# Reversing the tile order of the second half of the tokens at both ends of a stage

## The chip, the cores and the metric

The kernel runs on one core of a Trainium2 chip. The metric is the device time of one launch in microseconds. Before the change it is 2606.45 us, the median of 3 runs from 2605.48 to 2608.71. Engines are named TensorE (PE, with its weight loads as PEld), VectorE (DVE), ScalarE (ACT), GpSimd (POOL) and SyncE (SP), which issues the DMAs.

## The reference

One inference step of a decoder trunk of two layers, in float32, for 512 prompt tokens and 8 sample tokens that share the weights. Each layer is a half-step SwiGLU FFN, a token mixer with three parallel branches, and a second FFN, each with a residual and a layer norm:

```python
def _layer(x, prev, n_prev_valid, lb, p):
    x = _layernorm(ALPHA * x + 0.5 * _swiglu(x, p['ffn1_wg'], p['ffn1_wu'], p['ffn1_wd']), p['ln1_g'], p['ln1_b'])
    y, new_state = _mixer(x, prev, n_prev_valid, lb, p)
    x = _layernorm(ALPHA * x + y, p['ln2_g'], p['ln2_b'])
    x = _layernorm(ALPHA * x + 0.5 * _swiglu(x, p['ffn2_wg'], p['ffn2_wu'], p['ffn2_wd']), p['ln3_g'], p['ln3_b'])
    return x, new_state
```

The model width is 1024, the FFN's 2816. In the mixer one projection `h = x @ w_in + b_in` feeds sliding-window attention, a Mamba-2 scan and HGRN2 (a gated recurrence with 4 heads of 128, in chunks of 64 tokens), and three gates. The branches' gated results are summed and projected by `w_out`. The new states are outputs too.

## The kernel before, in words

Activations lie with features on the 128 partitions and 520 tokens along the free axis: a tensor of 1024 features is 8 tiles of 128 x 520. The tokens go in two halves of 260 (`HALVES`). A product of a 128 x 128 weight block and 260 tokens keeps float32 accuracy by splitting both sides into a high and a low part: three matmuls (L177, L178, L179 in `gemm`). A unit of weights is 128 x 1024: one DMA of 512 KB into `ws`, a cast to the high part `wh` on ScalarE (L90), a subtraction for the low part `wl` on VectorE (L91). `ws`, `wh` and `wl` have 5 buffers each, and `get` issues two units ahead of the one in use. One unit against one half of the tokens is 24 products.

A stage is an FFN or a mixer. At its end (`ln_tail`) all 8 output tiles are made for half 0 and then all 8 for half 1, so that the layer norm of half 0 runs while TensorE is at half 1; each of the 8 weight units is therefore loaded twice. The next stage begins in the same way: the FFN takes its first HEAD = 4 gate and up tiles for half 0 and then for half 1 (`halves_head`), the mixer its first ten units of `w_in` (`MIX_HEAD`). The layer norm of half 1 is kept back in `open_ln` and is finished inside the head (`ln_rest`: after the second gate product of an FFN, after the third unit of a mixer). `ln_apply` then writes the normed activations tile by tile: a subtraction on GpSimd (L248), a scaling on VectorE (L249), the high part `xh` on ScalarE (L252), the low part `xl` on VectorE (L253). The FFN's second kind of gate and up product (`gate_up`, matmuls L409 to L411) needs sums of activations, made by `combine` (VectorE L379, L387, L388, L393, GpSimd L380, ScalarE L392; results `sx`), and pairs of units from which VectorE (L102, L103) and GpSimd (L104, L105) make sums that are then cast and split (L73, L74). The values of a head pass through L318 to L320.

In the mixer, units 0 to 3 of `w_in` are the forget gates `hT` of the four HGRN heads (evacuated at L517), units 4, 5 and 6 the query, input and output gate of head 0, 7 to 9 those of head 1, 10 to 15 those of heads 2 and 3. After the mixer's head the rest comes in rounds, woven with the HGRN heads (`weave`, `HG_ROUNDS` = 0, 2, 4, 5). A head (`hgrn_head`) takes two sigmoids of its `hT` (L639, L640), cumulated products of eight on GpSimd, scaled queries `hep` and keys `hk` (L660, L661), then five levels, each a small group of four matmuls (L678) and multiplications on VectorE (L697, L698, L705, L706); transpositions of `hi` and `hk` (L717), states `hst` (L724, L725, L728), the output products (L735, L738), a reciprocal root by Newton steps on four columns (L262 to L267, `newton`), `ho` (L746), its transposition (L754) and `hy` (L756), cast to `yhh` (L535). The merge of the HGRN branch multiplies `yhh`.

The order on each engine is set by a list scheduler with a model of times: instructions are emitted in program order with priorities (`EARLY`: weights and evacuations before the rest), and each engine then runs its list in order.

Of the kernel before, what the change touches and what calls it, by code (L numbers as in the profile page):

```python
# [37 lines left out]
TAIL = 8  # L38
# [4 lines left out]
HEAD = 4  # L43
# [82 lines left out]
class Kernel:  # L126
# [59 lines left out]
    def ln_add(self, half, n, end=False):  # L186
        nc = self.nc
        c0, c1 = HALVES[half]
        w = c1 - c0
        y = self.y[n][:, c0:c1]  # L190
        s1, s2 = self.s1[half][:, :w], self.s2[half][:, :w]
        if n == 0:
# [8 lines left out]
        nc.vector.tensor_tensor(s1, self.y[0][:, c0:c1] if n == 1 else s1, y, op=ALU.add)  # L201
        if not end:
            nc.gpsimd.tensor_tensor(s2, s2, sq, op=ALU.add)

# [79 lines left out]
    def ffn_units(self, l, f):  # L284
        for j0, n in FFN_GROUPS:
            head = self.halves_head() if j0 == 0 else []
            for j, half in head:
                self.w.add(self.ap["w_gu"][l, f, j0 + j, 0], DT, P)
                self.w.add(self.ap["w_gu"][l, f, j0 + j, 1], DT, P)
            for j in range(HEAD if j0 == 0 else 0, n):  # L290
                self.w.add_pair(self.ap["w_gu"][l, f, j0 + j, 0], self.ap["w_gu"][l, f, j0 + j, 1])
            for m, half in self.halves_last(j0 + n == NFT):
                self.w.add(self.ap["w_dn"][l, f, m, :, j0 * P : (j0 + n) * P], n, P)

    @staticmethod
    def halves_head():

        return [(j, (0,)) for j in range(HEAD)] + [(j, (1,)) for j in range(HEAD)]

    @staticmethod  # L300
    def halves_last(last):

        if not last:
            return [(m, (0, 1)) for m in range(DT)]
        k = DT - TAIL
        return [(m, (0, 1)) for m in range(k)] + [(m, (0,)) for m in range(k, DT)] + [(m, (1,)) for m in range(k, DT)]

    def ffn(self, l, f, g, b, last=False, then=None):
        nc = self.nc
        sx = None  # L310
        for j0, n in FFN_GROUPS:
            hid = [(self.out_slot(F32R, "hh"), self.slot(F32R, "hl")) for _ in range(n)]

            def hidden(j, half, s, up):

                c0, c1 = HALVES[half]
                h, (hh, hl) = s, hid[j]
                nc.vector.scalar_tensor_tensor(h, up, 0.5, s, op0=ALU.mult, op1=ALU.mult)  # L318
                nc.scalar.copy(hh[:, c0:c1], h)
                nc.vector.tensor_tensor(hl[:, c0:c1], h, hh[:, c0:c1].bitcast(F32), op=ALU.subtract)  # L320

            for j, halves in self.halves_head() if j0 == 0 else []:
                wg, wu = self.w.get(), self.w.get()
                for half in halves:
                    pg, pu = self.bank(), self.bank()
                    self.gemm(pg, wg, self.xs, half)
                    if sx is None and j == 1:
                        self.ln_rest()
                        sx = self.combine()
                    self.gemm(pu, wu, self.xs, half)  # L330
                    with self.early(1):
                        s = self.half_tile()
                        nc.scalar.activation(s, pg[:, :TA], AF.Silu)
                        hidden(j, half, s, pu[:, :TA])
            self.gate_up(range(HEAD if j0 == 0 else 0, n), sx, hidden)
            if j0 == 0 and then:
                then()
            fin = j0 + n == NFT
            if j0 == 0:
                self.new_y()  # L340

            def down(m, wt, half):
                c0, c1 = HALVES[half]
                w = c1 - c0
                p = self.bank()
                self.gemm(p, wt, hid, half)
                y = self.y[m][:, c0:c1]
                with self.early(1):
                    if j0 == 0:
                        self.residual(m, half, p)  # L350
                    else:
                        nc.vector.tensor_tensor(y, y, p[:, :w], op=ALU.add)

            if not fin:
                for m, halves in self.halves_last(False):
# [100 lines left out]
    def ln_tail(self, step, g, b, bd, last=False):  # L456
        self.ln_begin(0)
        self.ln_begin(1)
        for m, halves in self.halves_last(True):
            wt = self.w.get()  # L460
            for half in halves:
                step(m, wt, half)
                with self.early(2):
                    self.ln_add(half, m, last and half == 1 and m == DT - 1)
                if m == DT - 1:
                    end = lambda half=half: self.ln_end(half, g, b, split=not last, out=self.ap["y"] if last else None)
                    if half == 0 or last:
                        end()
                    else:
                        self.open_ln = end  # L470
        y = self.y
        self.raw = (lambda n, half: y[n][:, slice(*HALVES[half])]), b, bd


    def mixer_units(self, l):
        w, ap = self.w, self.ap

        def win(*us):
            for u in us:
                w.add(ap["w_in"][l, u], DT, P)  # L480

        def branch(r):
# [12 lines left out]
        branch(2)  # L495
        for m, halves in self.halves_last(True):
            w.add(ap["w_out"][l, m], DT, P)

# [8 lines left out]
    def lin(self, evac, m=P, halves=(0, 1)):  # L507
        wt = self.w.get()
# [7 lines left out]
    def lin_bias(self, out, bias, scale=1.0, halves=(0, 1)):  # L516
        self.lin(lambda p, c0, c1: self.nc.scalar.activation(out[:, c0:c1], p, AF.Identity, bias=bias, scale=scale), halves=halves)  # L517

    def lin_silu(self, out, hbias, halves=(0, 1)):
# [10 lines left out]
        self.lin(evac, halves=halves)  # L530

    def split(self, y, name, slot=None):
        nc = self.nc
# [67 lines left out]
    def hgrn_lin(self, l):  # L601
# [2 lines left out]
        T = [self.slot(name="hT") for _ in range(HGH)]  # L604
        q, it, sg = {}, {}, {}

        def unit(u, halves=(0, 1)):
            hb = dp[:, u : u + 1]
            if u < 4:
                self.lin_bias(T[u], pr[:, 48 + u : 49 + u], halves=halves)  # L610
                return
            h, kind = (u - 4) // 3, (u - 4) % 3
            d, n = ((q, "hq"), (it, "hi"), (sg, "hsg"))[kind]
            if h not in d:
                d[h] = self.slot(name=n)
            if kind == 1:
                self.lin_bias(d[h], pr[:, 48 + u : 49 + u], halves=halves)
            else:
                self.lin_silu(d[h], hb, halves)

        for half in (0, 1):
            for u in self.MIX_HEAD:
                unit(u, (half,))
                if half == 0 and u == 2:
                    self.ln_rest()
        yield T, q, it, sg
        for u in range(16):
            if u in self.MIX_HEAD:
# [915 lines left out]
```

## Time and profile before

| | |
|---|---|
| Median of 3 runs | 2606.45 us (2605.48 to 2608.71) |
| The profiled execution's own time | 2604.06 us |
| Its span from first to last instruction | 2602.3 us |
| Mean granted clock of TensorE | 0.992 |
| TensorE busy | 2543.6 us, 98% of the span |
| VectorE busy | 1949.4 us, 75% |
| ScalarE, GpSimd busy | 48%, 27% |
| DMA | 314.86 MB in the main queue, 36.3% of 16 engines |
| Weight units of one kind (L90, L91) | 382 |

The busy shares are averages over stages with different limits. An engine's row in a view of stretches tells how full it is there, and the granted clock tells whether TensorE ran at its upper level. A timeline row has its start, its duration, the instruction's engine, line and tiles, and in brackets how long the engine stood idle before it and what released it. In a timeline a matmul of two float32 operands that are not split is counted twice, and neighbouring instructions of one line share a row.

### The profile page before, as it was taken

What the parts mean: (1) busy time and instruction counts of PE and PEld (TensorE: products, weight loads), DVE (VectorE), ACT (ScalarE), POOL (GpSimd) and SP (SyncE); (2) the same over time, 40 slices, a digit from 0 to 9 for tenths busy, and PEclk for the clock granted to TensorE, in tenths of its full rate; (3) what the DMA queues carried; (4) which work ended last, traced back from release to release, by engine and by line L of the source; (5) the groups of instructions that cost most, each with busy time, mean ns of one, the idle gap of its engine ahead of it and who ended that gap; (6) DMA issues with size and microseconds to landing.
All of it is one profiled execution on the core that took longest, in us unless ns stands there. A gap on an engine that the chain in (4) does not pass through costs nothing.

```text
span 2602.3 us, 51878 instructions
## 1 busy us (share of the span) xinstructions
PE 2543.6 (98%) x20784; PEld 2474.7 (95%) x20784; DVE 1949.4 (75%) x3690; ACT 1250.4 (48%) x2358; POOL 694.6 (27%) x635
## 2 busy tenths in 40 slices
PE   8999999999999999999999999999999999999997
PEld 8999999898989999999989999999989899999997
DVE  8795988864685598868897858989546845978586
ACT  6352566443534473434663524764435344635255
POOL 1121243300143441212331212433001434413124
PEclk9999999999999999999999999999999999999999
DMA  6332356412242343232532414564123423333233
GB/s 208 105 122 82 127 178 217 149 68 83 99 141 91 122 138 106 90 114 82 186 128 93 141 55 150 171 219 145 57 84 112 139 90 122 138 98 107 89 125 119
DMA packets 134066, 318.17 MB, mean 122 GB/s; under 512 B 20452, under 2 KB 56516, under 8 KB 133824
## 3 DMA queue, kind: packets, MB, share of 16 engines
q1 hardware_dynamic: 133824, 314.86, 36.3%
q8 instruction: 163, 2.67, 0.4%
q14 instruction: 79, 0.65, 0.1%
HBM read 302.93 MB, written 11.88 MB: 121 GB/s over the span
## 4 chain that ended last, share of the span: by engine, by line
PE 73%; DVE 15%; DMA 4%; issue 3%; ACT 3%; POOL 3%; SPq 0%; POOLq 0%; ACTq 0%; DVEq 0%
PE g L177 15%; PE g L178 15%; PE g L179 15%; PE g L409 5%; PE g L411 5%; PE g L410 5%; DVE wl L91 3%; PE s L409 2%; PE s L411 2%; PE s L410 2%; DMA ws<-in_w_gu 1%; PE s L1130 1%; DVE y L249 1%; DMA smp<-r8d 1%; DVE xl L253 1%
## 5 line engine op out<-in xcount | busy, mean ns | idle before, releaser
L177 PE MATMUL g<-xh,wh 128*128 128x260 f32 (+1 forms) x2336 | 669.1, 287 | 7.5 <-ACT xh L1407 5.7
L178 PE MATMUL g<-xl,wh 128*128 128x260 f32 (+1 forms) x2336 | 668.7, 286 | 3.6 <-DVE xl L253 2.7
L179 PE MATMUL g<-xh,wl 128*128 128x260 f32 (+1 forms) x2336 | 668.2, 286 | 1.9 <-DVE wl L91 1.9
L90 ACT CAST wh<-ws 128x1024 fp32r<-128x1024 f32 (+1 forms) x382 | 389.9, 1024 | 376.6 <-PE g L178 252.4
L91 DVE TENSOR_TENSOR wl<-ws,wh 128x1024 fp32r<-128x1024 f32 (+1 forms) x382 | 469.4, 1231 | 117.4 <-ACT wh L90 116.6
L177 PEld LDWEIGHTS g<-xh,wh 128*128 128x128 f32 (+1 forms) x2336 | 439.5, 188 | 17.5 <-issue 6.1
L178 PEld LDWEIGHTS g<-xl,wh 128*128 128x128 f32 (+1 forms) x2336 | 439.2, 188 | 12.0 <-issue 4.2
L179 PEld LDWEIGHTS g<-xh,wl 128*128 128x128 f32 (+1 forms) x2336 | 439.6, 188 | 9.5 <-issue 4.1
L73 ACT CAST wh<-ws 128x1024 fp32r<-128x1024 f32 (+1 forms) x288 | 265.4, 942 | 295.9 <-PE g L178 161.7
L179 PE MATMUL g<-hh,wl 128*128 128x260 f32 x1408 | 396.1, 283 | 0.0
L178 PE MATMUL g<-hl,wh 128*128 128x260 f32 x1408 | 396.0, 283 | 0.0
L177 PE MATMUL g<-hh,wh 128*128 128x260 f32 x1408 | 391.8, 282 | 1.6 <-DVE y L275 1.6
L74 DVE TENSOR_TENSOR wl<-ws,wh 128x1024 fp32r<-128x1024 f32 (+1 forms) x288 | 320.3, 1118 | 87.1 <-ACT wh L73 86.0
L105 POOL TENSOR_TENSOR ws<-ws 128x512 f32<-128x512 f32 x72 | 136.2, 1892 | 632.0 <-DMA ws<-in_w_gu 260.0
L177 PEld LDWEIGHTS g<-hh,wh 128*128 128x128 f32 x1408 | 263.0, 188 | 2.1 <-DVE y L275 2.0
L178 PEld LDWEIGHTS g<-hl,wh 128*128 128x128 f32 x1408 | 264.7, 188 | 0.1
L179 PEld LDWEIGHTS g<-hh,wl 128*128 128x128 f32 x1408 | 264.6, 188 | 0.2
L409 PE MATMUL g<-xh,wh 128*128 128x260 f32 x864 | 246.3, 286 | 2.6 <-ACT wh L73 2.5
L410 PE MATMUL g<-xl,wh 128*128 128x260 f32 x864 | 245.0, 284 | 0.0
L411 PE MATMUL g<-xh,wl 128*128 128x260 f32 x864 | 242.4, 284 | 1.9 <-DVE wl L74 1.9
L409 PEld LDWEIGHTS g<-xh,wh 128*128 128x128 f32 x864 | 164.4, 190 | 4.8 <-ACT wh L73 3.7
L409 PE MATMUL g<-sx,wh 128*128 128x260 f32 x576 | 164.7, 286 | 4.3 <-ACT wh L73 4.3
(407 smaller groups left out, 5721.6 us busy)
## 6 DMA issues: line engine op xcount, KB each, us to landing
ws<-in_w_gu SPq DMA_DIRECT2D x208, 512.0 KB
ws<-in_w_in SPq DMA_DIRECT2D x132, 512.0 KB
ws<-in_w_dn SPq DMA_DIRECT2D x96, 512.0 KB
ws<-in_w_out SPq DMA_DIRECT2D x32, 512.0 KB
ws<-in_w_dn SPq DMA_DIRECT2D x32, 384.0 KB
smp<-r8d SPq DMA_DIRECT2D x48, 256.0 KB
ws<-in_w_br SPq DMA_DIRECT2D x24, 512.0 KB
smp<-in_hgr SPq DMA_DIRECT2D x16, 256.0 KB
```

What stands on the lines that cost most here:

```text
L73: nc.scalar.copy(h[:, :n], s[:, :n])
L74: nc.vector.tensor_tensor(lo[:, :n], s[:, :n], h[:, :n].bitcast(F32), op=ALU.subtract)
L90: nc.scalar.copy(h[:, :n], s[:, :n])
L91: nc.vector.tensor_tensor(lo[:, :n], s[:, :n], h[:, :n].bitcast(F32), op=ALU.subtract)
L105: nc.gpsimd.tensor_tensor(pa[:, b], u[:, a], u[:, b], op=ALU.add)
L177: nc.tensor.matmul(out, lhsT=h[:, wc], rhs=xh[:, c0:c1], start=st, stop=False)
L178: nc.tensor.matmul(out, lhsT=h[:, wc], rhs=xl[:, c0:c1], start=False, stop=False)
L179: nc.tensor.matmul(out, lhsT=lo[:, wc], rhs=xh[:, c0:c1], start=False, stop=en)
L249: nc.vector.scalar_tensor_tensor(y, y, gn, rb, op0=ALU.mult, op1=ALU.mult)
L409: nc.tensor.matmul(out, lhsT=h[:, wc], rhs=xh, start=first and k == 0, stop=False, **go)
L410: nc.tensor.matmul(out, lhsT=h[:, wc], rhs=xl, start=False, stop=False, **go)
L411: nc.tensor.matmul(out, lhsT=lo[:, wc], rhs=xh, start=False, stop=k == HK - 1, **go)
```

## The change

In the second half of the tokens the tiles are taken in reverse order, both in the tails and in the heads (`there_and_back`). The last tile of half 0 is then the first of half 1, and its weights are kept instead of loaded again: the last pair of units in an FFN's head (`held` = 1), the last two units in a tail and in a mixer's head (`held` = 2). The sums of the layer norm follow the order in which the tiles come (`seen`). The units to be loaded fall from 382 to 358; the matmuls stay the same.

```diff
+    def there_and_back(tiles, held=1):
+        tiles = list(tiles)
+        back = tiles[::-1]
+        return [(t, 0, True) for t in tiles] + [(t, 1, k >= held) for k, t in enumerate(back)]
+
+    def halves_head(self):
+        return self.there_and_back(range(HEAD))
+
+    def halves_last(self):
+        return self.there_and_back(range(DT), 2)
...
-            for j, halves in self.halves_head() if j0 == 0 else []:
-                wg, wu = self.w.get(), self.w.get()
-                for half in halves:
-                    pg, pu = self.bank(), self.bank()
-                    self.gemm(pg, wg, self.xs, half)
...
+            held = {}
+            for j, half, new in self.halves_head() if j0 == 0 else []:
+                if new:
+                    held[j] = self.w.get(), self.w.get()
+                wg, wu = held[j]
+                pg, pu = self.bank(), self.bank()
+                self.gemm(pg, wg, self.xs, half)
...
-        for m, halves in self.halves_last(True):
-            wt = self.w.get()
-            for half in halves:
-                step(m, wt, half)
...
+        for m, half, new in steps:
+            if new:
+                held[m] = self.w.get()
+            step(m, held[m], half)
+            seen[half].append(m)
...
-        win(*self.MIX_HEAD, *self.MIX_HEAD)
+        win(*[u for u, _, new in self.there_and_back(self.MIX_HEAD, 2) if new])
...
-        for half in (0, 1):
-            for u in self.MIX_HEAD:
-                unit(u, (half,))
-                if half == 0 and u == 2:
-                    self.ln_rest()
+        held = {}
+        for u, half, new in self.there_and_back(self.MIX_HEAD, 2):
+            if new:
+                held[u] = self.w.get()
+            unit(u, (half,), held[u])
+            if half == 0 and u == 2:
+                self.ln_rest()
```

The lines of the changed kernel are numbered 1 to 12 higher (L91 stays, L253 is L254, L393 is L398, L517 is L527, L639 is L651, L678 is L690, L754 is L766).

The first place is VectorE at the turn to the second half in the head of the second FFN of layer 0. The rows are the last before the first addition L103 of a pair; `ws`, `wh`, `wl` are weights, `sx` are sums of activations, `ht` and `hl` values of the head's tiles. Before:

```order
L102 TENSOR_TENSOR ws<-ws 128x512
L388 SCALAR_TENSOR_TENSOR y<-y,par_1046 128x260
L91 TENSOR_TENSOR wl<-ws,wh 128x1024
L393 TENSOR_TENSOR sx<-y,sx 128x260 x2
L74 TENSOR_TENSOR wl<-ws,wh 128x512
L393 TENSOR_TENSOR sx<-y,sx 128x260 x3
L91 TENSOR_TENSOR wl<-ws,wh 128x1024
L318 SCALAR_TENSOR_TENSOR ht<-g,ht 128x260
L393 TENSOR_TENSOR sx<-y,sx 128x260
L320 TENSOR_TENSOR hl<-ht,hh 128x260 x4
L103 TENSOR_TENSOR ws<-ws 128x512
L74 TENSOR_TENSOR wl<-ws,wh 128x1024
```

After:

```order
L323 TENSOR_TENSOR hl<-ht,hh 128x260 x3
L91 TENSOR_TENSOR wl<-ws,wh 128x1024
L102 TENSOR_TENSOR ws<-ws 128x512
L398 TENSOR_TENSOR sx<-y,sx 128x260 x5
L91 TENSOR_TENSOR wl<-ws,wh 128x1024
L321 SCALAR_TENSOR_TENSOR ht<-g,ht 128x260
L323 TENSOR_TENSOR hl<-ht,hh 128x260
L74 TENSOR_TENSOR wl<-ws,wh 128x1024
L103 TENSOR_TENSOR ws<-ws 128x512
L321 SCALAR_TENSOR_TENSOR ht<-g,ht 128x260
L323 TENSOR_TENSOR hl<-ht,hh 128x260 x2
```

From the last `xl` of the layer norm on there are five L91 ahead of L103 before and three after (the last two of each stand here); one 1024-wide L74 has moved ahead of L103.

The second place is ScalarE at the first sigmoid of HGRN head 0 in layer 0; `hT` are the forget gates, `hk` the sigmoid's result, `hi` an input projection, `ht` the two parts of a query or output gate. Before:

```order
L517 ACTIVATE hi<-g,par_1046 128x260
L90 CAST wh<-ws 128x1024
L526 ACTIVATE ht<-g,dp_1048 128x260
L527 ACTIVATE ht<-g,dp_1048 128x260
L90 CAST wh<-ws 128x1024
L517 ACTIVATE hT<-g,par_1046 128x260
L639 ACT_TABLE_LOAD
L639 ACTIVATE hk<-hT 128x520
L640 ACTIVATE hT<-hT 128x520
L90 CAST wh<-ws 128x1024
```

After:

```order
L527 ACTIVATE hT<-g,par_1034 128x260
L90 CAST wh<-ws 128x1024
L527 ACTIVATE hT<-g,par_1034 128x260
L90 CAST wh<-ws 128x1024
L527 ACTIVATE hT<-g,par_1034 128x260
L90 CAST wh<-ws 128x1024
L527 ACTIVATE hT<-g,par_1034 128x260
L651 ACT_TABLE_LOAD
L651 ACTIVATE hk<-hT 128x520
L652 ACTIVATE hT<-hT 128x520
L536 ACTIVATE ht<-g,dp_1036 128x260
```

The sigmoid stood behind the first `hT` of the second half, and now stands behind four of them, which come last.

The third place is TensorE near the end of the HGRN heads in layer 0; L754 (then L766) transposes a `ho`, L678 (then L690) is a level's row, L717 (then L729) transposes `hi` or `hk`, L796 (then L808) and L1213 (then L1225) belong to the sample tokens; `g<-xh,wh` rows are products of projections. Before:

```order
L754 MATMUL s<-ident,ho 128x128 x4
L678 MATMUL s<-hep,hk 64x64 x4
L178 MATMUL g<-xl,wh 128x260
L179 MATMUL g<-xh,wl 128x260
L177 MATMUL g<-xh,wh 128x260
L796 MATMUL x<-ssq,inv_hg 128x32
L178 MATMUL g<-xl,wh 128x260
L179 MATMUL g<-xh,wl 128x260
L177 MATMUL g<-xh,wh 128x260
L178 MATMUL g<-xl,wh 128x260
L678 MATMUL s<-hep,hk 128x64 x4
```

After:

```order
L690 MATMUL s<-hep,hk 128x64 x4
L766 MATMUL s<-ident,ho 128x128 x4
L690 MATMUL s<-hep,hk 64x64 x4
L690 MATMUL s<-hep,hk 128x64 x4
L729 MATMUL s<-ident,hi 128x128 x4
L808 MATMUL x<-ssq,inv_hg 128x32
L729 MATMUL s<-ident,hk 128x128 x4
L177 MATMUL g<-yhh,wh 128x260
L690 MATMUL s<-hep,hk 128x64 x4
L1225 MATMUL x<-ident,s_av 8x128
L736 MATMUL s<-hit,hkt 128x128 x4
```

Of the eleven rows in the first list seven are products of projections between the small groups; in the second list one product is left.

## Rows read from the trace of the kernel before

**Rows 1.** The page's busy times by engine: busy us, share, instructions.

```profile
PE 2543.6 (98%) x20784; PEld 2474.7 (95%) x20784; DVE 1949.4 (75%) x3690; ACT 1250.4 (48%) x2358; POOL 694.6 (27%) x635
```

**Rows 2.** Stretches: span, busy time by engine (x instructions), granted clock, DMA share, GB/s.

```profile
core 0: us, PE busy (x) PEld busy (x) DVE busy (x) ACT busy (x) POOL busy (x), PEclk, DMA share, GB/s
...
957.00:987.00 30.00, 25.99 (x197) 24.12 (x195) 29.51 (x52) 16.99 (x36) 11.16 (x7) 0.97 0.30 104
...
985.00:1000.00 15.00, 14.23 (x91) 13.63 (x92) 12.14 (x16) 7.15 (x12) 2.59 (x2) 0.77 0.33 94
1345.00:1357.00 12.00, 8.68 (x54) 7.63 (x53) 11.52 (x18) 4.52 (x8) 4.10 (x2) 0.87 0.27 90
2275.00:2290.00 15.00, 13.84 (x89) 13.24 (x90) 12.20 (x17) 7.18 (x12) 2.62 (x2) 0.77 0.33 85
986.00:992.00 6.00, 5.75 (x25) 5.14 (x25) 6.00 (x7) 2.25 (x5) 1.31 (x2) 0.50 0.24 67
993.00:999.00 6.00, 6.00 (x52) 6.00 (x52) 3.73 (x5) 3.10 (x5) 0.00 (x0) 1.00 0.44 131
515.50:539.20 23.70, 23.32 (x201) 22.71 (x202) 19.06 (x67) 10.82 (x34) 1.27 (x1) 1.00 0.19 64
```

**Rows 3.** TensorE's waits, 955 to 990 us: total, times, longest.

```profile
PE g L409 <- ACT wh L73: 1.4, 1, 1.4
PE g L178 <- DVE xl L253: 0.9, 1, 0.9
PE g L411 <- DVE wl L74: 0.6, 1, 0.6
```

**Rows 4.** Timeline of VectorE, GpSimd, ScalarE at that turn: start, duration.

```profile
981.33 1.23 DVE L74 TENSOR_TENSOR wl<-ws,wh 128x1024 fp32r<-128x1024 f32 x1
982.47 0.78 DVE L393 TENSOR_TENSOR sx<-y,sx 128x260 fp32r<-128x260 f32 x2
...
981.56 2.83 POOL L104 TENSOR_TENSOR ws<-ws 128x512 f32<-128x512 f32 x1 [10.73 <-DMA ws<-in_w_gu]
984.96 1.28 POOL L105 TENSOR_TENSOR ws<-ws 128x512 f32<-128x512 f32 x1 [0.57 <-DMA ws<-in_w_gu]
...
984.42 2.94 ACT L73 CAST wh<-ws 128x1024 fp32r<-128x1024 f32 x3 [4.56 <-POOL ws L104]
```

**Rows 5.** TensorE's waits, 505 to 560 us.

```profile
PE s L678 <- DVE hk L698: 2.4, 1, 2.4
PE s L754 <- DVE ho L746: 0.4, 1, 0.4
```

**Rows 6.** Timeline of TensorE and VectorE around the first level row.

```profile
422.84 1.05 PE L678 MATMUL s<-hep,hk 128*128 128x128 f32 x8
...
420.71 0.42 DVE L661 TENSOR_TENSOR hep<-hq,hv 128x256 f32<-128x256 f32 x1
```

**Rows 7.** Timeline of TensorE, VectorE, ScalarE, 515 to 558 us.

```profile
515.52 1.08 PE L678 MATMUL s<-hep,hk 128*128 128x64 f32 x8 [2.37 <-DVE hk L698]
...
548.22 0.38 PE L738 MATMUL s<-hst,hep 128*128 128x128 f32 x2
...
538.44 0.69 DVE L746 TENSOR_TENSOR ho<-s,hr 128x512 f32<-128x512 f32 x1
...
552.25 1.23 DVE L91 TENSOR_TENSOR wl<-ws,wh 128x1024 fp32r<-128x1024 f32 x1 [0.29 <-ACT wh L90]
...
553.58 0.69 DVE L746 TENSOR_TENSOR ho<-s,hr 128x512 f32<-128x512 f32 x1
...
556.76 0.75 DVE L756 SCALAR_TENSOR_TENSOR hy<-s,par,hsg 128x512 f32<-128x512 f32 x1 [2.48 <-PE s L754]
...
557.67 0.62 ACT L535 CAST yhh<-hy 128x512 fp32r<-128x512 f32 x1
```

**Rows 8.** Timeline of VectorE and GpSimd, 505 to 519 us.

```profile
508.14 2.33 DVE L91 TENSOR_TENSOR wl<-ws,wh 128x1024 fp32r<-128x1024 f32 x1
...
508.09 1.29 POOL L786 TENSOR_TENSOR smp<-smp 128x512 f32<-128x512 f32 x1 [1.96 <-DVE newton L265]
```

More of the change, by code (lines that the diff above doesn't have):

```diff
@@ L184, in ln_begin, with ln_add @@
         self.s2 = {**getattr(self, "s2", {}), half: self.half_tile()}
-    def ln_add(self, half, n, end=False):
+    def ln_add(self, half, seen, end=False):
         nc = self.nc
@@ L189, in ln_add @@
         w = c1 - c0
-        y = self.y[n][:, c0:c1]
+        first, y = (self.y[seen[k]][:, c0:c1] for k in (0, -1))
         s1, s2 = self.s1[half][:, :w], self.s2[half][:, :w]
-        if n == 0:
+        if len(seen) == 1:
             nc.scalar.activation(s2, y, AF.Square)
@@ L200, in ln_add @@
             nc.scalar.activation(self.lnc, sq[:, :1], AF.Ln, bias=self.ones[:, :1], scale=0.0)
-        nc.vector.tensor_tensor(s1, self.y[0][:, c0:c1] if n == 1 else s1, y, op=ALU.add)
+        nc.vector.tensor_tensor(s1, first if len(seen) == 2 else s1, y, op=ALU.add)
         if not end:
@@ L286, in ffn_units @@
             head = self.halves_head() if j0 == 0 else []
-            for j, half in head:
-                self.w.add(self.ap["w_gu"][l, f, j0 + j, 0], DT, P)
-                self.w.add(self.ap["w_gu"][l, f, j0 + j, 1], DT, P)
+            for j, _, new in head:
+                for k in (0, 1) if new else ():
+                    self.w.add(self.ap["w_gu"][l, f, j0 + j, k], DT, P)
             for j in range(HEAD if j0 == 0 else 0, n):
                 self.w.add_pair(self.ap["w_gu"][l, f, j0 + j, 0], self.ap["w_gu"][l, f, j0 + j, 1])
-            for m, half in self.halves_last(j0 + n == NFT):
-                self.w.add(self.ap["w_dn"][l, f, m, :, j0 * P : (j0 + n) * P], n, P)
+            for m, _, new in self.halves_last() if j0 + n == NFT else [(m, 0, True) for m in range(DT)]:
+                if new:
+                    self.w.add(self.ap["w_dn"][l, f, m, :, j0 * P : (j0 + n) * P], n, P)
     @staticmethod
[L296 to L306, printed above, removed]
+    def there_and_back(tiles, held=1):
[6 more added lines that the diff above has]
+        return self.there_and_back(range(DT), 2)
     def ffn(self, l, f, g, b, last=False, then=None):
@@ L320, in hidden @@
                 nc.vector.tensor_tensor(hl[:, c0:c1], h, hh[:, c0:c1].bitcast(F32), op=ALU.subtract)
[L322 to L334 removed]
+            held = {}
[5 more added lines that the diff above has]
+                self.gemm(pg, wg, self.xs, half)
+                if sx is None and j == 1:
+                    self.ln_rest()
+                    sx = self.combine()
+                self.gemm(pu, wu, self.xs, half)
+                with self.early(1):
+                    s = self.half_tile()
+                    nc.scalar.activation(s, pg[:, :TA], AF.Silu)
+                    hidden(j, half, s, pu[:, :TA])
             self.gate_up(range(HEAD if j0 == 0 else 0, n), sx, hidden)
@@ L354, in ffn @@
             if not fin:
-                for m, halves in self.halves_last(False):
+                for m in range(DT):
                     wt = self.w.get()
-                    for half in halves:
+                    for half in (0, 1):
                         down(m, wt, half)
@@ L458, in ln_tail @@
         self.ln_begin(1)
-        for m, halves in self.halves_last(True):
-            wt = self.w.get()
-            for half in halves:
-                step(m, wt, half)
[L463 to L470, printed above, removed]
+        held, steps = {}, self.halves_last()
+        seen = {0: [], 1: []}
+        for m, half, new in steps:
[3 more added lines that the diff above has]
+            seen[half].append(m)
+            end = len(seen[half]) == DT
+            with self.early(2):
+                self.ln_add(half, seen[half], last and half == 1 and end)
+            if end:
+                rest = lambda half=half: self.ln_end(half, g, b, split=not last, out=self.ap["y"] if last else None)
+                if half == 0 or last:
+                    rest()
+                else:
+                    self.open_ln = rest
         y = self.y
@@ L495, in mixer_units @@
         branch(2)
-        for m, halves in self.halves_last(True):
-            w.add(ap["w_out"][l, m], DT, P)
+        for m, _, new in self.halves_last():
+            if new:
+                w.add(ap["w_out"][l, m], DT, P)
     MIX_HEAD = (0, 1, 2, 3, 4, 5, 6, 7, 8, 9)
@@ L505, in sm, with lin @@
         return self.small.tile([rows, cols], dt, tag=name, name=name, bufs=bufs)
[L507 to L508 removed]
+    def lin(self, evac, m=P, halves=(0, 1), wt=None):
+        wt = wt or self.w.get()
         for half in halves:
```

19 lines of the change are left out of this document (10 added, 9 removed).

## The prediction

> **What bounds the kernel now.** First the page's line of busy time: TensorE is busy 98% of the span, VectorE 75%, the others far less [rows 1]. The change takes no matmul away, so it can win only from TensorE's idle time and from stretches in which the clock is low, and it can lose wherever TensorE gets work too early. The next view is the one by stretches of time. Around the turn from the first to the second half of the tokens in three of the four FFNs (the first FFN of layer 0 has no layer norm before it) VectorE is full: in the first of them 29.5 of 30 us, while TensorE idles 4.0 us; in the 12 to 15 us behind each turn the granted clock averages 0.77, 0.87 and 0.77 [rows 2]. Inside the first of these, 6 us at a granted clock of 0.50 (the 1.2 GHz level) hold 25 matmuls, and 6 us at 1.00 (2.4 GHz) hold 52 [rows 2]; so a matmul of 260 columns takes 0.115 us of TensorE at the upper level. The list of waits says what TensorE stood for there: a cast of a paired weight, 1.4 us, an xl of the layer norm, 0.9, a paired weight's low part, 0.6 [rows 3].
>
> The second place is the mixer behind its head, where four HGRN heads, each a chain of small operations on VectorE, ScalarE, GpSimd and TensorE, lie between the products of the projections. Today they are nearly hidden: 2.4 and 0.4 us of waits between 505 and 560 us [rows 5]. What hides them is the number of products between two links of a chain, and that is what the change's order moves.
>
> **The FFN turns (three places).** VectorE decides. Counted from the last xl, the first addition of a pair (L103) stands behind five subtractions of weight units (L91) today and behind three then: the fewer loads of the head. An undisturbed L91 takes 1.23 us [rows 7], so 2.46 us go; one subtraction of a pair (L74, 1.23) and two of the sx (L393, 0.78 together) move ahead of it [rows 4]. Net 2.46 - 1.23 - 0.78 = 0.45 us. Next on that path is GpSimd's L104, 2.83 us while L74 runs beside it; the like addition L105, begun 3.4 us later, takes 1.28 [rows 4]. With L74 already done, L104 should take about the same: 1.55 less. The cast that TensorE waits for starts when L104 ends (984.42) [rows 4]. So it comes 0.45 + 1.55 = 2.0 us earlier, against 1.4 + 0.6 us of waits that it can remove [rows 3]: I take 2.0 us a turn. Bounds: 0.45 us if L104 stays long, and 4.0 us if all idle time of the 30 us stretch goes, which needs the xl wait to go too; nothing in the order speaks for that. What is late next is the xl (0.9 us). Three turns: -6.0 us, between -1.4 and -12.
>
> The clock is another matter. By the mean granted clock the three stretches lose 0.23 x 15, 0.13 x 12 and 0.23 x 15 = 3.4 + 1.6 + 3.4 = 8.5 us [rows 2]. Since the xl wait and part of the others stay, I count nothing of it in the forecast, and up to 8.5 us in the range.
>
> **The tails and the loads.** 24 of 382 weight units go (each a 512 KB DMA, a cast and an L91). In the tails TensorE runs on products alone and these engines have room, so I cost it at nothing; cover is TensorE itself. The price if that were wrong is on the side of the held tiles: two of five buffers of the cast weights are kept through the turn, so later casts might start late. Two held units give 2 x 24 products = 5.5 us of TensorE, more than an L91 (1.23 [rows 7]) and a cast (2.94 us for three, 0.98 [rows 4]) together, so nothing here either.
>
> **The mixers' heads (two places).** T of head 0, the forget gate's projection, is the first unit, so its second half was the first of the second half's units and becomes the last. The sigmoid on it stood right behind that unit; nine units of 24 products, 216 products, go ahead of it: about 25 us. The rounds of projections that follow do not move back with it. In TensorE's order the first level row of the first head comes only 186 products later. So its chain loses 30 products or 3.5 us of cover. Before, its operand hep is ready at 421.13 and the row starts at 422.84, 1.7 us of room [rows 6]. Loss 1.8 by these rows, nothing if an L91 less in between (1.23) and the like make the chain shorter, 3.5 if the room is spent: I take 1.0.
>
> At the end the fourth head's chains meet a fixed point, the merge with the first branch's weights, and the delay cannot be passed on. From the second level row of the fourth head to the transposition of the third head's ho TensorE has 134 products and some 13 groups of small matmuls before; then 39 products and the same groups. Before, this took from 515.52 to the end of ho at 539.13: 23.6 us [rows 7], with TensorE 23.3 us busy [rows 2], of which 134 x 0.115 = 15.4 are products and 7.9 the small groups. Then TensorE has 39 x 0.115 + 7.9 = 12.4 us of work there. The chain itself needs between its VectorE work, 19.06 us less two L91 that fall out [rows 2, 7], 16.6, and the whole 23.6 us of before. Bare are 4.2 to 11.2 us. Below that, nothing at all if VectorE has done a part ahead. I take 5.0, near the row that counts VectorE's own work, since it is the engine with the most to do there; range 0 to 11.2.
>
> The fourth head's ho: from the last of its products with the state (548.60) over the Newton steps to the end of L746 (554.27) it took 5.7 us, one L91 of 1.23 in it [rows 7]. Cover was 64 products, now 12, 1.4 us. Bare: 5.7 - 1.4 - 1.23 = 3.1 (0 if other rows are moved ahead, 4.3 with the L91). Then hy (0.75) and its cast yhh (0.62) before the first merge product [rows 7]: 0 to 1.4, I take 1.0. From this the waits of before come off, 2.4 + 0.4 [rows 5], as these stand in the same rows. One mixer: 1.0 + 5.0 + 3.1 + 1.0 - 2.8 = +7.3; two: +14.6, between -5.6 (all waits go, none comes) and +35 (3.5 + 11.2 + 4.3 + 1.4 - 2.8 = 17.6 each).
>
> One rule of the Trainium skill speaks against counting small. The trace has an L91 of 2.33 us at 508.14 beside GpSimd's L786 of 1.29 at 508.09, where the other at 552.25 is 1.23 [rows 7, 8]. The page "SBUF — State Buffer", section "Who interferes with whom", says that only the port pair shared by VectorE and GpSimd brings contention, as an exclusive lock. By it the L91 waits out the L786 whole; 1.23 + 1.29 = 2.5 agrees with the 2.33 roughly, and each such meeting in a bare chain would add about 1.1 us.
>
> **Sum.** -6.0 + 14.6 = +8.6 us against the profiled execution's 2604.06; that lies 2.39 below the median of 2606.45 to which the change is compared, so 2606.45 + 8.6 = 2615.0 us.
>
> **Rivals.**
> - *Delay mostly hidden, turns and clock won (faster).* If the scheduler's order lets the HGRN chains catch up in the rounds before the merge, a mixer costs 2 us; the turns give 6 and most of the clock, 6 more. 2 x 2 - 6 - 6 = -8: 2598. For it: the waits of before are small, the clock falls just behind the waits that go. Against it: the first xl wait stays, and bare rows at the end have nothing to fill them.
> - *They cancel.* 3 us a mixer, -6 at the turns: 2606. For it: the lower end of the bare rows (nothing to 4.2), and that a part of the 2.8 us comes off twice.
> - *The mixers clearly slower.* One mechanism: in the bare rows each level needs VectorE's two multiplications and a copy before TensorE's next small group, and GpSimd's sample work holds VectorE meanwhile as at 508 us [rows 8]; bare rows then cost near their upper end, 11.2 instead of 5.0: 13.5 a mixer. 27 - 6 = +21, and if TensorE falls to 1.2 GHz behind such a gap, about 2 more: 2629. It decides once the bare part passes about 8 us a mixer. For it: 23.6 us is what the chain took with cover. Against: with cover, the chain had no hurry.
> - *The change does not do what it says*: fewer loads are in the order of the engines (358 L91 for 382), so I give it no chance.
>
> **Chances.** Forecast 0.40 (its own range 2611.7 to 2622), faster rival 0.18, no change 0.26, clearly slower 0.16. A measurement of this kernel tells 0.2% (5.2 us) from no change, so the limits are 2601.2 and 2611.7: faster 0.18, within 0.27 (the rival that cancels and a sliver of the forecast), slower 0.55. The range of 8 in 10 runs from 2599, in the faster rival, to 2631, behind the slow one.
>
> **What would show it.** At the FFN turns L104 near 1.3 us and the cast before TensorE reaches it: wait for L73 gone; xl's wait stays; granted clock in the 15 us after still under 0.9. In the mixers TensorE's waits behind the head grow from 2.8 to about 10 us, on the operands of the level rows (hk, hep) and on ho. A tail with new waits for casts would disprove the cost of nothing for the held tiles. The forecast is wrong if the mixers' waits stay under 5 us, or if the clock after the turns stays at 1.00.

## The result and the profile after

The changed kernel takes 2639.91 us (median of 4 runs, 2638.50 to 2645.41) against 2606.34 us before: a ratio of 1.0131, 95% interval 1.0114 to 1.0149. It is slower by 33.6 us where 8.6 were forecast, and it lies above the range of 2599 to 2631. The profiled execution took 2640.79 us with a span of 2639.0. The page's line of busy times, which answers to [rows 1]:

```profile
PE 2563.7 (97%) x20784; PEld 2490.3 (94%) x20784; DVE 1936.7 (73%) x3666; ACT 1226.8 (46%) x2334; POOL 656.3 (25%) x635
```

Matmuls are as many as before. The span grew by 36.7 us: TensorE's idle time from 2602.3 - 2543.6 = 58.7 to 2639.0 - 2563.7 = 75.3 us (+16.6), its busy time by 20.1 us for the same work. The second part is slower matmuls: the stretches in which the granted clock was at 1.2 GHz add up to 42.0 us before and 82.8 us after (some 11 us of each stand at the kernel's end), and half of the difference is 20.4.

Where it was lost shows when both traces are cut at the same product, counted from the start (the 3000th and 5000th product of 260 columns around the first mixer, the 12,900th and 15,000th around the second). The view by stretches, first the kernel before:

```profile
core 0: us, PE busy (x) PEld busy (x) DVE busy (x) ACT busy (x) POOL busy (x), PEclk, DMA share, GB/s
377.00:707.90 330.90, 322.06 (x2598) 301.71 (x2597) 228.65 (x582) 167.87 (x424) 65.14 (x94) 0.99 0.39 127
1703.50:2058.40 354.90, 347.11 (x2785) 323.60 (x2784) 252.37 (x664) 161.86 (x419) 78.67 (x103) 0.99 0.38 124
```

The changed kernel:

```profile
376.20:722.40 346.20, 329.06 (x2598) 307.50 (x2597) 234.81 (x580) 165.67 (x422) 61.30 (x94) 0.97 0.37 118
1715.20:2095.60 380.40, 361.76 (x2785) 335.91 (x2785) 254.34 (x662) 163.21 (x421) 75.54 (x103) 0.94 0.37 116
```

The first mixer lost 15.3 us: 8.3 more idle (8.84 to 17.14) and 7.0 more busy. The second lost 25.5: 10.9 more idle (7.79 to 18.64) and 14.6 more busy. The three FFN turns, cut in the same way (the 6800th to the 7200th product of 260 columns, the 9750th to the 10,100th, the 16,400th to the 16,800th), add up in the view by stretches to these sums, first the kernel before, then the changed one:

```profile
sum 164.70, PE 151.70 PEld 145.47 DVE 153.16 ACT 96.81 POOL 46.83; mean PE 50.57 PEld 48.49 DVE 51.05 ACT 32.27 POOL 15.61
```

```profile
sum 154.70, PE 145.00 PEld 139.45 DVE 144.22 ACT 90.65 POOL 39.73; mean PE 48.33 PEld 46.48 DVE 48.07 ACT 30.22 POOL 13.24
```

They won 10.0 us (3.7, 2.6 and 3.7): 3.3 of idle time (13.0 to 9.7) and 6.7 of busy time, which is clock. The rest, -0.8 at the start and +6.7 between, lies outside the mixers and the turns; a stretch of 6.8 us at 1.2 GHz at 766 us, which the profile of before does not have, is part of it.

In the first mixer, 405 to 605 us, the waits of TensorE, which answer to [rows 5], are these (total us, times, longest); they sum to 17.1 us, where the kernel before has 8.1 in the same stretch:

```profile
PE s L766 <- DVE ho L758: 5.5, 2, 3.1
PE s L690 <- DVE hk L718: 3.7, 3, 2.1
PE s L690 <- DVE hk L710: 3.6, 3, 1.6
PE g L177 <- ACT ht L1288: 1.9, 1, 1.9
PE g L177 <- ACT yhh L553: 1.9, 1, 1.9
PE s L750 <- DVE hst L740: 0.5, 1, 0.5
```

They are mostly the rows of the HGRN heads: level rows on `hk` and the transpositions of `ho`. The wait on `yhh` is one of the merge's products, but for the sample tokens' 8 columns (L553, at 556.23), not for a head's own cast (L545). TensorE's timeline of the bare rows, answering to [rows 7] (the lines between are products):

```profile
540.65 0.95 PE L766 MATMUL s<-ident,ho 128*128 128x128 f32 x4 [3.11 <-DVE ho L758]
541.53 3.02 PE L690 MATMUL s<-hep,hk 128*64 128x64 f32 x16
544.34 1.06 PE L729 MATMUL s<-ident,hi 128*128 128x128 f32 x4
...
556.23 0.39 PE L177 MATMUL g<-yhh,wh 128*128 128x260 f32 x1 [1.86 <-ACT yhh L553]
...
573.27 1.08 PE L766 MATMUL s<-ident,ho 128*128 128x128 f32 x4 [2.35 <-DVE ho L758]
```

And the clock there, in two stretches that lie wholly at 1.2 GHz:

```profile
541.00:551.00 10.00, 9.98 (x49) 8.97 (x47) 7.05 (x21) 2.19 (x5) 0.00 (x0) 0.50 0.17 56
571.60:581.60 10.00, 8.33 (x31) 6.51 (x32) 5.68 (x20) 2.15 (x3) 0.00 (x0) 0.50 0.24 94
```

TensorE stood for `ho` until 540.65, the granted clock fell to 0.50 at 540.8 and stayed there for 10.2 us; again from 571.5 for 10.2 us. Among the heads of the second mixer there are six such stretches, 41 us in all. Each begins in a wait of TensorE of 1.7 to 3.1 us or up to 1.5 us behind one.

The chain itself can be read off ScalarE. The first sigmoid of the heads in the kernel before and in the changed one (calls, durations in ns, first and last start), and the last cast `yhh` of the first mixer in the timeline of the changed one:

```profile
L639 ACT ACTIVATE hk<-hT x8: 629/647/658, 407.5 to 1778.9; 128x520 f32<-128x520 f32 x8
```

```profile
L651 ACT ACTIVATE hk<-hT x8: 627/640/659, 432.5 to 1819.8; 128x520 f32<-128x520 f32 x8
```

```profile
575.18 0.62 ACT L545 CAST yhh<-hy 128x512 fp32r<-128x512 f32 x1 [5.40 <-DVE hy L768]
```

The first sigmoid starts 25.0 us later, as reckoned (216 products at 0.115 are 24.8). The last `yhh` of the first mixer starts at 575.18 where it was 557.67 [rows 7]: 17.5 us later. So the chain of four heads shrank only from 150.2 to 142.7 us. Most of the late start arrived at the end of the chain.

At the FFN turns VectorE, GpSimd and the cast moved as forecast. At the first of them, the timeline of GpSimd, VectorE and ScalarE (compare [rows 4]):

```profile
996.75 1.29 POOL L104 TENSOR_TENSOR ws<-ws 128x512 f32<-128x512 f32 x1 [9.45 <-DVE ws L103]
...
994.47 0.41 DVE L323 TENSOR_TENSOR hl<-ht,hh 128x260 fp32r<-128x260 f32 x1
...
996.88 1.78 DVE L323 TENSOR_TENSOR hl<-ht,hh 128x260 fp32r<-128x260 f32 x2
...
998.07 2.95 ACT L73 CAST wh<-ws 128x1024 fp32r<-128x1024 f32 x3 [0.67 <-POOL ws L104]
```

TensorE's waits there (compare [rows 3]):

```profile
PE g L178 <- DVE xl L254: 0.9, 1, 0.9
PE g L414 <- ACT wh L73: 0.6, 1, 0.6
PE g L179 <- DVE wl L91: 0.6, 2, 0.3
PE s L414 <- ACT wh L73: 0.4, 1, 0.4
```

And the stretch behind the turn (compare [rows 2]):

```profile
985.00:1000.00 15.00, 13.52 (x107) 12.69 (x105) 14.86 (x27) 7.05 (x16) 2.71 (x2) 1.00 0.19 70
```

L104 takes 1.29 us for 2.83, the wait for L73 is 0.6 + 0.4 for 1.4, and the clock behind the turn stays at 1.00 where it was 0.77 [rows 2]. Counted from the last `xl` (959.17 before, 975.12 after), the cast L73 starts 2.3 us earlier, where 2.0 were forecast.

### The profile page after: what moved, and what is told of

It is laid out like the page before. It is cut to its first block, busy times and chain, and to the rows that moved or that the text cites. A ratio compares the mean times of both kernels' runs of the same rounds, so it can differ in the third digit from the quotient of the medians.

```text
span 2639.0 us, 51721 instructions
## 1 busy us (share of the span) xinstructions
PE 2563.7 (97%) x20784; PEld 2490.3 (94%) x20784; DVE 1936.7 (73%) x3666; ACT 1226.8 (46%) x2334; POOL 656.3 (25%) x635
## 4 chain that ended last, share of the span: by engine, by line
PE 74%; DVE 15%; DMA 4%; issue 3%; ACT 3%; POOL 2%; SPq 0%; POOLq 0%; ACTq 0%; DVEq 0%
PE g L177 16%; PE g L178 16%; PE g L179 16%; PE g L414 5%; PE g L416 5%; PE g L415 5%; PE s L414 2%; PE s L416 2%; DVE wl L91 2%; PE s L415 2%; DMA ws<-in_w_gu 2%; PE s L1142 1%; DVE wl L74 1%; ACT wh L73 1%; DVE y L250 1%
## 5 line engine op out<-in xcount | busy, mean ns | idle before, releaser
L91 DVE TENSOR_TENSOR wl<-ws,wh 128x1024 fp32r<-128x1024 f32 (+1 forms) x358 | 437.1, 1223 | 148.6 <-ACT wh L90 147.3
L90 ACT CAST wh<-ws 128x1024 fp32r<-128x1024 f32 (+1 forms) x358 | 364.9, 1023 | 380.7 <-PE g L178 277.4
L73 ACT CAST wh<-ws 128x1024 fp32r<-128x1024 f32 (+1 forms) x288 | 265.4, 941 | 293.9 <-PE g L178 160.3
L74 DVE TENSOR_TENSOR wl<-ws,wh 128x1024 fp32r<-128x1024 f32 (+1 forms) x288 | 322.5, 1126 | 89.4 <-ACT wh L73 87.5
L105 POOL TENSOR_TENSOR ws<-ws 128x512 f32<-128x512 f32 x72 | 123.2, 1711 | 640.7 <-DVE wl L91 236.9
```

The costliest lines, as they stand in the source:

```text
L73: nc.scalar.copy(h[:, :n], s[:, :n])
L74: nc.vector.tensor_tensor(lo[:, :n], s[:, :n], h[:, :n].bitcast(F32), op=ALU.subtract)
L90: nc.scalar.copy(h[:, :n], s[:, :n])
L91: nc.vector.tensor_tensor(lo[:, :n], s[:, :n], h[:, :n].bitcast(F32), op=ALU.subtract)
L105: nc.gpsimd.tensor_tensor(pa[:, b], u[:, a], u[:, b], op=ALU.add)
```

## The experiments

The times are medians, the intervals those of the ratio to the kernel before; 0.2% is 5 us. Each kernel was profiled in one of its runs.

**The mixer's head put back, all else changed.** `mix_steps` replaces `there_and_back` there:

```diff
+    def mix_steps(self):
+        return [(u, half, True) for half in (0, 1) for u in self.MIX_HEAD]
```

> The mixer's head as before (second half forward, all ten units loaded twice), tails and FFN heads reversed and held as in the change. Theory (the order in the mixer's head costs the time: head 0's forget gate comes last, the HGRN heads lose their cover, TensorE waits and its clock falls): the loss of 17.5 us in the first mixer and 24 us in the second goes, what the FFN turns gain stays: about 2606.3 - 5 = 2601 us (2597 to 2604), TensorE's waits in the mixers as before (8.1 and 5.8 us), clock at 1.00 there but for one dip in layer 1. Rival (held tiles keep two of five buffers and later casts come late, in tails as in heads): most of the loss stays, 2615 us or more.

Measured 2599.71 us (0.9964 to 0.9985): faster than before, as expected. The waits of the first mixer are near those of before again, 9.3 us for 8.1:

```profile
PE s L693 <- DVE hk L713: 5.4, 3, 2.6
PE s L693 <- DVE hk L721: 2.2, 3, 1.2
PE x L784 <- DVE s_q L780: 1.2, 1, 1.2
PE s L753 <- DVE hst L740: 0.5, 1, 0.5
```

The loss sits in the mixer's head, and holding tiles in tails and FFN heads does not cause it.

**Only the mixer's head changed.** The kernel before with the change's loop in `hgrn_lin` and its list in `mixer_units`, nothing else.

> Only the mixer's head changed (reversed, two units held), FFN heads and tails as before. Theory: 2606.3 + 41.5 = 2648 us (2643 to 2653), with the FFN turns at the lower clock as before. Rival (the tails or FFN heads bring part of the loss): below 2630 us.

Measured 2648.79 us (1.0150 to 1.0178), +42.5: the time is as expected. The two halves add up: +42.5 and -6.6 make 35.9 for 33.6. The expected low clock behind the FFN turns did not come. At the first turn TensorE waits for the casts as it did before (967.4 to 1022.6 us):

```profile
PE g L414 <- ACT wh L73: 1.4, 1, 1.4
PE g L416 <- DVE wl L74: 0.9, 2, 0.6
```

And yet the granted clock is 1.00 throughout all three turns. Between the same products as above they take:

```profile
sum 159.70, PE 145.91 PEld 139.43 DVE 152.66 ACT 97.14 POOL 46.62; mean PE 48.64 PEld 46.48 DVE 50.89 ACT 32.38 POOL 15.54
```

That is 5.0 us less than before, with idle time up by 0.8 and busy time down by 5.8. So these waits alone do not decide whether the clock falls at a turn.

**Same loads, old order of the second half.** Half 0 backwards, half 1 forwards, two units held:

```diff
+    def mix_steps(self):
+        return self.there_and_back(self.MIX_HEAD[::-1], 2)
```

> As the change, but in the mixer's head half 0 goes over the units backwards (9 to 0) and half 1 forwards (0 to 9), so two units are held and eight loaded as in the change while half 1 has the order of before. Theory: the price is the order of half 1 alone, so the time is that of the kernel with the old mixer head, about 2601 us (2597 to 2604). Rival (holding two units in the mixer's head costs): 2615 us or more.

Measured 2600.03 us (0.9965 to 0.9983), as expected: neither holding two units in the mixer's head nor its turning back costs, the order of half 1 does.

**One unit moved, from both sides.** On the kernel with the FFN heads alone, with all loads, unit 0 goes last in half 1; on the change, unit 0 goes first in half 1 and the rest stays reversed:

```diff
+        return [(u, 0, True) for u in self.MIX_HEAD] + [(u, 1, True) for u in (*self.MIX_HEAD[1:], 0)]
...
+        return self.there_and_back((*self.MIX_HEAD[1:], 0), 2)
```

> On the kernel with only the FFN heads changed (2596.0): in the mixer's head unit 0 alone, the forget gate of head 0, is moved to the end of half 1 (1 to 9, then 0); nothing is held, all ten units are loaded twice. Theory (the place of this one unit sets when the HGRN heads begin, and with it waits and clock): 2596 + 42 = 2638 us (2632 to 2644), low-clock stretches in both mixers as in the change (some 20 and 40 us long). Rival (the whole reversed order, the late queries and input gates, or the held tiles make the price): under 2610 us.

> The change with one unit moved: in the mixer's head half 0 goes 1 to 9 and then 0, half 1 goes 0 and then 9 down to 1; two units held, eight loaded, as in the change. Theory: the forget gate of head 0 is early again and the loss goes, about the 2600 us of the kernels with the old order of half 1 (2598 to 2606; the query of head 0 still comes five units later, which may cost some us). Rival (the reversed order as such costs): 2620 us or more.

Measured 2639.05 us (1.0103 to 1.0136), +43.0 against the FFN heads alone, and 2598.27 us (0.9959 to 0.9981). Both as expected. This one unit, the forget gate of head 0, makes the whole loss and takes it away.

**The unit in the middle.** Half 1 as 1 to 5, 0, 6 to 9, on the kernel with the FFN heads alone:

```diff
+        return [(u, 0, True) for u in self.MIX_HEAD] + [(u, 1, True) for u in (1, 2, 3, 4, 5, 0, 6, 7, 8, 9)]
```

> FFN heads changed, tails as before, all units loaded twice; in the mixer's head half 1 goes 1 to 5, 0, 6 to 9: the forget gate of head 0 comes five units later than in the kernel with the FFN heads alone, four earlier than with unit 0 last. Theory (a threshold: most small rows at the end still have products between them in this order, only the fourth head's ho has 13 products of cover for 64): 2596 + 2 x 3 = 2602 us (2598 to 2608), little low clock in the mixers. Rival (the loss grows evenly with the place): 2596 + 43 x 5/9 = 2620 us (2615 to 2625).

Measured 2618.75 us (1.0034 to 1.0066): +22.7 for five places where nine cost 43.0, 4.5 and 4.8 us a place. My theory of a threshold fell, its rival held. A place is 24 products, 2.8 us, in each of two mixers; 2.3 to 2.4 of them are paid. What is paid is waits and slower matmuls together, so it does not by itself say how much room the chain had.

**Only the FFN heads; only the tails; FFN heads with all loads.** All three keep the old head of the mixer. The first edit below leaves the tails as before (first and third kernel), the second the FFN heads (second kernel), the third reverses the FFN heads and holds nothing (third kernel):

```diff
+    def halves_last(self):
+        return [(t, half, True) for half in (0, 1) for t in range(DT)]
...
+    def halves_head(self):
+        return [(t, half, True) for half in (0, 1) for t in range(HEAD)]
...
+    def halves_head(self):
+        return self.there_and_back(range(HEAD), 0)
```

> Only the FFN heads reversed, with the last pair held; tails and mixer head as before. Theory: the gain sits at the three FFN turns (two L91 fewer ahead of L103, GpSimd's L104 alone, clock stays at 2.4 GHz): -5 us, 2601 us (2597 to 2604), L104 near 1.3 us and no stretch at 1.2 GHz behind the turns. Rival (the gain comes from the fewer loads of the tails, which end the stage before): 2606 us, clock low behind the turns as before.

> Only the tails reversed with two units held; heads of FFN and mixer as before. The kernel with the FFN heads alone took 2596.0 and with FFN heads and tails 2599.7: if the tails' change costs by itself, 2606.3 + 3.7 = 2610 us (2608 to 2613), a wait for a cast or for the next stage's weights in the tails. Rival (my first reckoning: nothing, the difference of the two is scatter or an interplay with the turns): 2606 us (2604 to 2608).

> FFN heads reversed but with nothing held: four pairs loaded twice as before; tails and mixer head as before. Theory (the gain at the turns is the two L91 that no longer stand ahead of L103): no gain, 2606 us (2603 to 2608), the waits for the cast L73 and the low clock behind the turns as before. Rival (the reversed order alone gives it): 2596 us (2593 to 2599).

The FFN heads alone: 2596.03 us (0.9951 to 0.9977), -10.3, the fastest median of all, below both kernels and below the expected range; twice the -5 of the theory. The tails alone: 2608.15 us (0.9999 to 1.0018); whether they cost 2 us, at the lower edge of the expected range, or nothing, as the rival has it, stays unclear. FFN heads reversed with four pairs loaded twice: 2606.26 us (0.9986 to 1.0005), no gain, as expected. Its trace has everything of before again: GpSimd's L104 beside L74, TensorE's wait for the cast, and the clock in the 6 us behind the turn.

```profile
981.44 2.83 POOL L104 TENSOR_TENSOR ws<-ws 128x512 f32<-128x512 f32 x1 [10.73 <-DVE ws L103]
```

```profile
PE g L417 <- ACT wh L73: 1.4, 1, 1.4
```

```profile
985.00:991.00 6.00, 5.46 (x22) 4.93 (x23) 5.63 (x7) 3.13 (x6) 1.31 (x2) 0.51 0.18 46
```

The kernel with the pair held, at the same place, GpSimd's timeline and the stretch:

```profile
979.29 1.29 POOL L104 TENSOR_TENSOR ws<-ws 128x512 f32<-128x512 f32 x1 [9.45 <-DVE ws L103]
```

```profile
980.00:986.00 6.00, 5.00 (x39) 4.56 (x38) 5.85 (x7) 3.52 (x5) 2.14 (x2) 1.00 0.26 90
```

With the two units not loaded the gain comes; the order alone gives none of it. How the clock comes with them is not settled: in none of the eleven profiles of kernels that hold the pair did it fall at a turn, and in three of the four with all loads it did, but in the fourth (only the mixer's head changed) it stayed at 1.00 with the same waits.

**FFN heads and a mixer's head that begins with unit 0.** The kernel with unit 0 first, with the old tails.

> FFN heads reversed with the last pair held, mixer's head with half 0 as 1 to 9, 0 and half 1 as 0, 9 down to 1 and two units held, tails as before. If the parts add up, the 2596.0 of the FFN heads alone and nothing or a microsecond from the mixer's head: 2595 us (2592 to 2598). Rival (only the whole with the tails makes the mixer's head neutral): 2600 us or more.

Measured 2598.25 us (0.9960 to 0.9982), a little above the expected range and below the rival's. Its runs (2593.6 to 2602.3) overlap those of the FFN heads alone (2593.1 to 2600.9): fewer loads in the mixer's head give nothing that can be measured.

**More work in the gaps.** On the change, behind each level row of the third and fourth head:

```diff
+            if h in (2, 3):
+                fill = self.bank("s")
+                for c in range(4):
+                    nc.tensor.matmul(fill[:, :P], lhsT=ks[:, :P], rhs=qp[:, c * P : (c + 1) * P], start=True, stop=True)
```

> The change with matmuls added that nothing reads: behind each of the five level rows of the third and fourth HGRN head four 128 x 128 float32 matmuls into a spare bank, some 10 us of TensorE work per mixer if TensorE never waited. Theory (TensorE falls to 1.2 GHz because the bare rows leave it idle, and that is the larger part of the loss): the low-clock stretches in the mixers, 61 us, shrink to under 30 and the time falls below the change, 2625 to 2638 us, although work is added. Rival (the clock does not depend on these gaps or the chain alone sets the time): 2645 to 2662 us with the low clock as before. The scheduler also moves products behind the added work, so the waits have to be read beside the clock.

Measured 2637.39 us (1.0100 to 1.0132; 2630.7 to 2639.2), against 2639.91 (1.0114 to 1.0149): the time is at the edge of what my theory asked, and the two intervals overlap, so the medians alone show no gain. The page's lines of its profiled execution, which was the fastest at 2630.70:

```profile
span 2628.9 us, 52040 instructions
...
PE 2566.1 (98%) x20944; PEld 2496.9 (95%) x20944; DVE 1931.2 (73%) x3666; ACT 1227.3 (47%) x2334; POOL 657.4 (25%) x635
```

Against the profile of the change the low-clock time fell from 82.8 to 54.9 us, 14 us of TensorE's time, and idle time from 75.3 to 62.8. Among the heads of the two mixers it fell from 61 to 31 us, just above the theory's 30. Busy time rose by 2.4 all the same, so the added matmuls took some 16 us, and this one execution is 10.1 us shorter than the profiled one of the change. That is in line with the gaps bringing the clock down; it does not show it, since the scheduler moved products too, nor does it say what the low clock alone costs.

**The heads pushed together.** The change with another table of starts, and the kernel with the FFN heads alone with the same table:

```diff
-HG_ROUNDS = (0, 2, 4, 5)
+HG_ROUNDS = (0, 1, 3, 4)
```

> The change with another table of starts for the HGRN heads: rounds 0, 1, 3, 4 in place of 0, 2, 4, 5, so that the later heads are emitted a round earlier; nothing else differs. In TensorE's order the first row of head 0 stays, the first level row of the fourth head stands 73 products earlier (8.4 us). Theory (the chain of four heads from the first sigmoid to the last hy sets when the merge can start; where the heads can be pushed together, the late start is made good): about 8 us less per mixer, 2623 us (2616 to 2632). Rival (the chain is VectorE's work one after the other and cannot be pushed together): 2636 us or more.

> The kernel with only the FFN heads changed (2596.0), with HGRN starts at rounds 0, 1, 3, 4 in place of 0, 2, 4, 5. In TensorE's order the last transposition of a ho stands 15 products earlier, the fourth head's first level row 6. Theory (the chain of heads is already at its edge in the old order, so that any later start is paid): some us less, 2592 us (2588 to 2595). Rival (in the old order the chain has slack, the table matters only once the start is late): 2596 us (2595 to 2600).

On the change 2618.78 us (1.0035 to 1.0061), 21 less, as expected. The first sigmoid stays late, the last `yhh` of the first mixer comes 6.3 us earlier than in the change (568.88 for 575.18):

```profile
L651 ACT ACTIVATE hk<-hT x8: 627/638/652, 433.1 to 1793.3; 128x520 f32<-128x520 f32 x8
```

```profile
568.88 0.62 ACT L545 CAST yhh<-hy 128x512 fp32r<-128x512 f32 x1 [5.16 <-DVE hy L768]
```

On the FFN heads alone it gave 2619.09 us (1.0035 to 1.0062), 23 more. The theory and its rival both missed: with that table the old order is as slow as the late one, so the place of unit 0 costs nothing measurable there any more. In the first mixer the time is lost between 424 and 506 us (all of its 9.7 us, by cuts at the same products), with TensorE's clock at 0.95 in one stretch where the old table had 1.00; first the kernel with the new table, 455 matmuls in 65 us, then the one with the old, 462 in 60:

```profile
440.00:505.00 65.00, 58.10 (x455) 55.60 (x456) 48.08 (x122) 30.29 (x96) 25.69 (x32) 0.95 0.56 166
```

```profile
440.00:500.00 60.00, 55.32 (x462) 53.43 (x461) 44.88 (x113) 29.83 (x95) 22.82 (x26) 1.00 0.53 168
```

Why the table costs 23 us in the old order is not settled. It does say that the start of the first head is not the only thing that sets a mixer's time, and that the price of a place of unit 0 holds for the old table. The old table and the old order of the units fit each other; that this is a matter of how the four heads stand between the products is argued, not shown.

## Why the prediction was wrong

The direction, the place and the first link were right: the sigmoid 25 us later, TensorE waiting on `hk` and `ho`, and the turns gaining. The step that failed is the sum over a mixer, "1.0 + 5.0 + 3.1 + 1.0 - 2.8 = +7.3", taken twice: the mixers lost 15.3 and 25.5 us.

- *The clock was left out of the mixers.* All four terms are idle time, with products priced at 0.115 us each. TensorE's additional idle time is 8.3 and 10.9 us, near the 7.3 and inside the bounds; its additional busy time, 7.0 and 14.6 us, has no term in the sum. Only the slow rival had one, "about 2 more", where 21.6 came. The trace of before had shown the lower clock behind the waits of an FFN turn, 25 matmuls in 6 us [rows 2]; I counted that, in the range, where it could be won and not where it could be lost. The Trainium skill, "TensorE: Matmul & The Clock Gate", section "A second HAM failure mode: psum-queue depth-cycling", tells of another kernel in which frequent short idling between groups of matmuls makes the clock swing between its levels; the second mixer, with six stretches at 0.50, agrees.
- *That the idle time came out near its sum is in part luck.* In the first mixer 4.7 us of waits stand at level rows between 450 and 467 us, where only the 1.0 of the first row was counted. The rows priced at 5.0 (537.5 to 560.6 us) idle 5.0, but as 3.1 on `ho` and 1.9 on the sample tokens' columns of `yhh`. The fourth head's `ho` came to 2.35 for 3.1. The last term, 1.0 for `hy` and `yhh`, came to nothing there, and 1.9 on `ht` (L1288) had no term.
- *The delay was priced by pieces, not as a whole.* 24.8 us of products change from behind the chain to ahead of it in each mixer, and 15.3 and 25.5 were lost. The runs with unit 0 at places 0, 5 and 9 show that 4.5 to 4.8 us of 5.5 a place are paid. This is another view of the same loss, not a second one beside the clock. What the delay would cost with the clock at its upper level throughout no run shows.

The rival "the mixers clearly slower" named the right outcome, at 2629, with another mechanism: it had GpSimd's sample work holding VectorE in the bare rows. In the stretch that was priced at 5.0 GpSimd is busy 1.26 of 23.1 us, and in the two stretches at the low clock shown above 0.00 of 10.

```profile
537.50:560.60 23.10, 18.12 (x117) 16.72 (x117) 16.15 (x58) 6.71 (x28) 1.26 (x1) 0.78 0.11 38
```

Whether its work before 537 us delayed the chain was not tested.

The turns: 2.0 us of waits each were forecast, -6.0, and nothing for the clock. They won 10.0, but only 3.3 of it is idle time. VectorE, GpSimd and the cast did what was forecast, and the kernel with all loads takes the gain back; the step that failed is that the earlier cast would take 2.0 of the 1.4 + 0.6 us of waits away, since waits of 0.6 and 0.4 remained. The other 6.7 us are the clock, which I gave to the faster rival: I argued that the remaining `xl` wait would keep it low, and it did not. L104 is where the Trainium skill bears on it: "SBUF — State Buffer", section "Who interferes with whom", has VectorE and GpSimd share a pair of ports as an exclusive lock. It agrees: L104 took 2.83 us beside an L74 [rows 4]; where it started first it took 1.29, and the two L323 beside it took 1.78 together for 0.41 each.

The tails and the held tiles were costed at nothing. For the held tiles of the mixer's head that is shown (same time with two held units or none); the tails may cost some 2 us.

## What to carry to other kernels

Where small chains are woven into a long row of products, price a moved producer first as a whole: the products that go from behind it to ahead of it, times their duration. With this kernel's table of starts 43.0 of 49.7 us so reckoned were paid, clock included; with another table nothing was, so the whole is a price to fear and not a law. Whoever adds up waits instead has to price them twice, once as idle time and once as slower matmuls (19.2 and 21.6 us here in two mixers), for losses as for gains. Reverse an order of tiles only where the next step takes them in any order; where a consumer begins with one tile, keep that tile first and turn around the others.

## What was not expected of the hardware

At the FFN turn two waits of 0.6 and 0.4 us for the casts left the clock at 1.00, while 1.4 us in one and 0.6 in another were followed by 1.2 GHz [rows 2, 3]; the xl wait of 0.9 stood ahead of both. It would be wrong to read a limit from this: with only the mixer's head changed the waits of 1.4 and 0.6 us were there at all three turns and the clock stayed at 1.00. Behind the bare rows of the first mixer the clock was at 0.50 for 10.2 us twice, although TensorE was busy 9.98 of 10 us in one of them: busy by the trace, with 49 matmuls in 10 us, many of them small.
